# The FFN's down projection: three pairs of row tiles by Strassen's seven products

## The chip, the cores and the metric

The kernel runs on one core of a Trainium2 chip. The metric is device time in microseconds (us) from one launch: TensorE (PE) multiplies matrices, VectorE (DVE) and ScalarE (ACT) work on tiles, GpSimd (POOL) adds at the side, and the queues of SyncE (SP) and ScalarE issue DMA transfers. A profiled execution of the same program gives the trace.

## The reference

Two layers of a decoder trunk, in float32, with 512 positions and width 1024. What the change touches is the second half of each layer and its surroundings:

```python
for l in range(DEPTH):                       # 2
    h = rmsnorm(x, norm_mix[l])
    ...                                      # four mixers, output projection, x = x + ...
    h = rmsnorm(x, norm_ffn[l])
    u = causal_dwconv(h @ ffn_up[l], ffn_dw[l], ffn_dw_b[l])     # 1024 -> 2 * 2816, 3 taps
    gate, val = split_cols(u, [2816, 2816])
    x = x + (silu(gate) * val) @ ffn_down[l]                     # 2816 -> 1024
return rmsnorm(x, norm_final)
```

## The kernel before, in words

Everything is kept transposed: a tile has 128 channels on the partitions and the 512 positions as columns. The residual `x` is eight such tiles. Products run in fp16 with a high and a low part of each operand: `mm3` (lines 231 to 236) issues three matmuls for one 128 x 128 weight block, high by high, high by low, low by high, and sums them in PSUM.

A weight piece is at most 128 x 1024 float32. `w_load` loads it from SP's queue into a staging buffer `st`; `_split` then makes its high part on ScalarE (line 211) and its low part on VectorE (line 212), both into `hl`. There are two staging buffers and five `hl` in the small ring; inside the FFN a second ring `fst`/`fhl` in the FFN's own pool adds two and four, and the third field of an item says which ring it takes. `weights` lists all pieces in order of use, `next_w` keeps `depth` of them split ahead of the one in use (2 in FFN up, 4 at the changes of stage), and splits are traced with high priority. All instructions are put in order per engine when the program is built, by a planner that goes through a simulated timeline with priorities; each engine then takes its own in that order.

FFN up (`ffn_up`): 22 pairs of row tiles, a gate tile and a value tile, each 8 blocks x 3 matmuls of 512 columns into one PSUM bank `g` (two of them). Lines 1103 to 1105 evacuate a bank with the three taps; lines 1109 to 1111 make silu(gate) * value; lines 1113 and 1114 split it into the high and low part of one `act` chunk of 128 x 512. The first four tiles come from `gemm_head`, which runs them in column halves behind the norm.

FFN down (`project`): for each of eight row tiles, 22 chunks x 3 matmuls into one bank; line 1028 (`back`) adds the result to `x`, and `norm_add` squares it for the next norm (ScalarE, then a sum on POOL). The last tile runs in two halves of 256 columns, so that the norm of the first half, or the output of the second layer (`finish`), can start while the second half is multiplied.

Of the kernel before, what the change touches and what calls it, by code (L numbers as in the profile page):

```python
# [40 lines left out]

FST, FHL = 2, 4
# [106 lines left out]
class Builder:  # L149
    def __init__(self, ctx, tc, a):  # L150
# [13 lines left out]
        self.ffn = self.spare = False  # L164
# [25 lines left out]
    def w_load(self, src, cols, ring):  # L190
        nc = self.nc
        if ring:
            st = self.fp.tile([128, 1024], F32, tag="fst", bufs=FST, name=self.n("st"))
        else:
            st = self.wst.tile([128, 1024], F32, tag="st", name=self.n("st"))
        nc.sync.dma_start(st[:, :cols], src)
        return st

# [4 lines left out]
    def _split(self, src, cols, ring=False):  # L203

        nc = self.nc
        st = self.w_load(src, cols, ring)
        if ring:
            hl = self.fp.tile([128, 2, 1024], F16, tag="fhl", bufs=FHL, name=self.n("hl"))
        else:
            hl = self.whl.tile([128, 2, 1024], F16, tag="hl", name=self.n("hl"))  # L210
        act = nc.scalar.activation(hl[:, 0, :cols], st[:, :cols], AF.Copy, scale=SW)  # L211
        dve = nc.vector.scalar_tensor_tensor(hl[:, 1, :cols], st[:, :cols], SW, hl[:, 0, :cols],  # L212
                                             op0=ALU.mult, op1=ALU.subtract)
        for later, earlier in zip((act, dve), self.after):
            self.order(later, earlier)
        return hl
# [14 lines left out]
    def mm3(self, ps, hl, kk, hx, cols, start, stop):  # L231
        nc = self.nc
        w = slice(kk * 128, kk * 128 + 128)
        nc.tensor.matmul(ps, hl[:, 0, w], hx[:, 0, cols], start=start, stop=False)  # L234
        nc.tensor.matmul(ps, hl[:, 0, w], hx[:, 1, cols], start=False, stop=False)  # L235
        nc.tensor.matmul(ps, hl[:, 1, w], hx[:, 0, cols], start=False, stop=stop)  # L236

    def gemm(self, hx):
        if self.stash:
            if self.ffn and len(self.ready) <= self.depth:  # L240
                self.prefetch()
            self.spare = self.ffn
            return self.stash.pop(0)
        hl = self.next_w()

        ps = self.rbank() if self.spare else self.gbank()
        self.spare = False
# [817 lines left out]
    def project(self, rhs, order, tail, scale, norm_eng):  # L1065
        nc = self.nc
        nk = len(order)

        def tile_(ps, hls, cols):
            for i, k in enumerate(order):  # L1070
                self.mm3(ps, hls[k // 8], k % 8, rhs[k], cols, i == 0, i == nk - 1)

        nw = (nk + 7) // 8
        full = slice(0, 512)
        for m in range(NK - tail):
            hls = [self.next_w() for _ in range(nw)]
            ps = self.gbank()
            tile_(ps, hls, full)
            self.back(m, ps, full, scale)
            self.norm_add(m, full, norm_eng)  # L1080
        self.depth = HEAD
        hls = [[self.next_w() for _ in range(nw)] for _ in range(tail)]
        for cols in self.HALVES:
            for i in range(tail):
                m = NK - tail + i
                ps = self.gbank()[:, 0:256]
                tile_(ps, hls[i], cols)
                self.back(m, ps, cols, scale)
                self.norm_add(m, cols, nc.vector if m < NK - 1 else None)
            yield cols  # L1090

    def ffn_up(self, fp, hx):
# [3 lines left out]
        acts = []  # L1096
        for i in range(NF):
            us = []
            for half in range(2):
                ch = i + NF * half  # L1100
                ps = self.gemm(hx)
                u = fp.tile([128, 512], F32, tag="u", bufs=4, name=self.n("u"))
# [5 lines left out]
            th = fp.tile([128, 512], F32, tag="fth", bufs=2, name=self.n("fth"))  # L1108
            nc.scalar.activation(th, us[0], AF.Tanh, scale=0.5)
            stt(us[0], th, 1.0, us[0], op0=ALU.add, op1=ALU.mult)  # L1110
            nc.vector.tensor_tensor(us[0], us[0], us[1], op=ALU.mult)  # L1111
            a = fp.tile([128, 2, 512], F16, tag="act", bufs=NF, name=self.n("act"))
            nc.scalar.copy(a[:, 0], us[0])  # L1113
            nc.vector.tensor_tensor(a[:, 1], us[0], a[:, 0], op=ALU.subtract)
            acts.append(a)
        return acts

    def weights(self):
        a = self.a
        items = []  # L1120
        for l in range(L):
# [13 lines left out]
            for m in range(2 * NF):  # L1135
                items.append((a["up"][l, m], 1024, m < HEAD or m % 2 == 1))
            for m in range(NK):
                for g in range(3):
                    k1 = min(8, NF - 8 * g) * 128
                    items.append((a["dn"][l, m, :, 1024 * g:1024 * g + k1], k1, m == NK - 1 or (3 * m + g) % 2 == 1))  # L1140
# [53 lines left out]
    def run(self):  # L1194
# [24 lines left out]
        for l in range(L):  # L1219
            with pool(f"vp{l}") as self.vp, pool(f"rp{l}") as self.rp:  # L1220
                self.mixers(hx, l, src)
            with pool(f"fp{l}") as fp:
                self.fp, self.ffn, self.depth = fp, True, HEAD
                self.norm_begin(fp)
                hf = self.new_hx(fp, "hf")
                for cols in self.out_second(OTAIL):
                    self.norm_apply(self.d["gf"], hf, cols)
                self.gemm_head(hf, HEAD)
                self.depth = 2
                acts = self.ffn_up(fp, hf)  # L1230
# [95 lines left out]
```

## Time and profile before

| | |
|---|---|
| time, median of 3 runs | 1348.35 us (1348.11 to 1351.59) |
| the profiled execution: its own time, its span | 1351.01 us, 1349.2 us |
| TensorE, VectorE, ScalarE, POOL busy | 1301.4, 903.1, 609.9, 117.7 us |
| mean granted clock of TensorE | 0.989 of full speed |
| loaded from HBM | 114.30 MB, 88 GB/s over the span |
| FFN down, first layer: first matmul, first matmul of the last tile's halves | 560.84 us, 660.56 us |

The busy time of an engine is a share of the whole span; what a change in one stage is worth is read in that stage. A matmul is listed with its full duration, although the next one starts before it ends: the distance from one start to the next is what counts.

### The profile page before, as it was taken

The page shows a single profiled execution, that of the slowest core. Times are in us where ns is not written, and L with a number is a line of the kernel's source. Part 1 is how long each engine was busy: PE and PEld are TensorE (multiplying, and loading weights), DVE is VectorE, ACT ScalarE, POOL GpSimd, SP SyncE. Part 2 cuts the span into 40 slices and gives each one's busy share as a digit, 9 for nine tenths or more (in the row PEclk, how much of TensorE's full clock was granted, in tenths as well). Part 3 has the DMA queues.
Part 4 walks back from the last instruction along what each step waited for, and adds up shares of the span by engine and source line. Part 5 has one row for each costly group of instructions (what it writes and reads, how often), then busy time and mean ns, then how long its engine had stood idle before and what let it go on. Part 6 is the DMA issues. An engine that isn't in the chain of part 4 may idle for free.

```text
span 1349.2 us, 22863 instructions
## 1 busy us (share of the span) xinstructions
PE 1301.4 (96%) x9198; PEld 738.1 (55%) x9198; DVE 903.1 (67%) x1770; ACT 609.9 (45%) x1115; POOL 117.7 (9%) x180
## 2 busy tenths in 40 slices
PE   5999999999999999999999998999999999999996
PEld 4545567657644444444674455775584444444445
DVE  6779985677876767732276899757768666666313
ACT  4544557654544444532154345766345444444210
POOL 2000022223000000001000001223020000000110
PEclk9999999999999999999998999998999999999998
DMA  6421310023223233453133223001213333336201
GB/s 221 157 85 60 118 33 10 1 71 110 78 94 110 94 109 95 141 167 121 52 101 107 80 78 103 10 3 32 94 51 109 107 96 108 96 103 188 70 28 63
DMA packets 41864, 119.96 MB, mean 89 GB/s; under 512 B 4896, under 2 KB 11680, under 8 KB 41760
## 3 DMA queue, kind: packets, MB, share of 16 engines
q1 hardware_dynamic: 35136, 110.50, 25.9%
q10 hardware_dynamic: 6624, 8.01, 1.8%
q8 instruction: 72, 1.18, 0.4%
q14 instruction: 32, 0.26, 0.1%
HBM read 114.30 MB, written 4.19 MB: 88 GB/s over the span
## 4 chain that ended last, share of the span: by engine, by line
PE 81%; DVE 12%; ACT 2%; DMA 2%; issue 2%; SPq 0%; DVEq 0%; ACTq 0%
PE g L234 21%; PE g L235 21%; PE g L236 21%; DVE cacc L755 4%; PE v L922 3%; PE t L911 2%; DVE hl L212 2%; PE s L891 2%; PE r L578 1%; PE r L234 1%; PE r L235 1%; PE r L236 1%; DVE e L894 1%; DMA st<-in_wi_dram 1%; ACT e L898 1%
## 5 line engine op out<-in xcount | busy, mean ns | idle before, releaser
L236 PE MATMUL g<-hx,hl 128*128 128x512 f16 (+1 forms) x1008 | 368.6, 367 | 0.0
L234 PE MATMUL g<-hx,hl 128*128 128x512 f16 (+1 forms) x1008 | 367.8, 367 | 0.8 <-DVE q L787 0.8
L235 PE MATMUL g<-hx,hl 128*128 128x512 f16 (+1 forms) x1008 | 368.2, 367 | 0.3 <-DVE hx L423 0.3
L212 DVE SCALAR_TENSOR_TENSOR hl<-st,hl 128x1024 f16<-128x1024 f32 (+2 forms) x200 | 238.6, 1195 | 115.8 <-ACT hl L211 114.2
L211 ACT ACTIVATE hl<-st 128x1024 f16<-128x1024 f32 (+2 forms) x200 | 204.4, 1026 | 213.4 <-PE g L236 149.3
L234 PEld LDWEIGHTS <-hl 128*128 128x128 f16 x1724 | 170.1, 99 | 159.5 <-issue 5.2
L236 PEld LDWEIGHTS <-hl 128*128 128x128 f16 x1724 | 169.3, 98 | 157.0 <-issue 2.2
L235 PEld LDWEIGHTS <-hl 128*128 128x128 f16 x1724 | 169.6, 98 | 154.2 <-issue 2.5
L235 PE MATMUL g<-act,hl 128*128 128x512 f16 (+1 forms) x396 | 140.7, 355 | 0.0
L236 PE MATMUL g<-act,hl 128*128 128x512 f16 (+1 forms) x396 | 140.7, 355 | 0.0
L234 PE MATMUL g<-act,hl 128*128 128x512 f16 (+1 forms) x396 | 140.7, 355 | 0.0
L1104 DVE SCALAR_TENSOR_TENSOR u<-g,d_fdw,u 128x511 f32<-128x511 f32 x82 | 61.5, 750 | 95.7 <-ACT u L1103 95.7
L1103 ACT ACTIVATE u<-g,par,d_fdw 128x512 f32<-128x512 f32 x82 | 63.7, 777 | 101.6 <-PE g L236 101.4
L755 DVE SCALAR_TENSOR_TENSOR cacc<-gl,d_cdw,cacc 128x511 f32<-128x511 f32 (+14 forms) x120 | 90.0, 750 | 1.3
L1028 DVE SCALAR_TENSOR_TENSOR x<-g,x 128x512 f32<-128x512 f32 (+1 forms) x62 | 34.9, 568 | 83.3 <-PE g L236 83.1
L909 POOL TENSOR_SCALAR e<-e,den 128x512 f32<-128x512 f32 (+3 forms) x96 | 55.9, 595 | 316.4 <-DVE den L901 207.4
L390 POOL TENSOR_TENSOR acc<-acc,sq 128x256 f32<-128x256 f32 (+1 forms) x38 | 41.7, 1098 | 462.4 <-ACT sq L383 405.5
L894 DVE CUSTOM_DVE_ANT_0 e<-s,con 128x512 f32<-128x512 f32 (+3 forms) x96 | 46.8, 488 | 34.2 <-PE s L891 24.4
L1113 ACT CAST act<-u 128x512 f16<-128x512 f32 x44 | 27.1, 617 | 93.2 <-DVE u L1111 93.2
L1105 DVE SCALAR_TENSOR_TENSOR u<-g,d_fdw,u 128x510 f32<-128x510 f32 x82 | 61.4, 748 | 2.8
L898 ACT ACTIVATE e<-e,mx 128x512 f32<-128x512 f32 (+3 forms) x96 | 53.1, 556 | 17.0 <-DVE mx L896 16.9
L383 ACT ACTIVATE sq<-x 128x256 f32<-128x256 f32 (+1 forms) x54 | 24.5, 467 | 74.9 <-DVE x L1028 71.1
(265 smaller groups left out, 1665.0 us busy)
## 6 DMA issues: line engine op xcount, KB each, us to landing
st<-in_up_dram SPq DMA_DIRECT2D x88, 512.0 KB, 3.5
st<-in_wi_dram SPq DMA_DIRECT2D x40, 512.0 KB, 3.4
st<-in_dn_dram SPq DMA_DIRECT2D x32, 512.0 KB, 3.7
st<-in_wo_dram SPq DMA_DIRECT2D x16, 512.0 KB, 3.5
st<-in_dn_dram SPq DMA_DIRECT2D x16, 384.0 KB, 3.2
w<-in_cw_dram ACTq DMA_DIRECT2D x16, 256.0 KB, 4.4
st<-in_wv_dram SPq DMA_DIRECT2D x8, 396.0 KB, 3.2
x<-in_x_dram SPq DMA_DIRECT2D x16, 128.0 KB, 3.4
```

The source lines that it names most:

```text
L211: act = nc.scalar.activation(hl[:, 0, :cols], st[:, :cols], AF.Copy, scale=SW)
L212: dve = nc.vector.scalar_tensor_tensor(hl[:, 1, :cols], st[:, :cols], SW, hl[:, 0, :cols], op0=ALU.mult, op1=ALU.subtract)
L234: nc.tensor.matmul(ps, hl[:, 0, w], hx[:, 0, cols], start=start, stop=False)
L235: nc.tensor.matmul(ps, hl[:, 0, w], hx[:, 1, cols], start=False, stop=False)
L236: nc.tensor.matmul(ps, hl[:, 1, w], hx[:, 0, cols], start=False, stop=stop)
L755: nc.vector.scalar_tensor_tensor(acc[:, s:512], gl[:, 0:512 - s], wj, acc[:, s:512], op0=ALU.mult, op1=ALU.add)
L894: nc.vector.tensor_tensor_reduce(es[i], ps[:, o:o + w], mask[:, 384 - 128 * t:512], op0=ALU.add, op1=ALU.max, scale=1.0, scalar=-3e38, acc ...
L898: nc.scalar.activation(es[i], es[i], AF.Exp, scale=SC, bias=mx[:, i:i + 1], accum_out=den[:, i:i + 1])
L909: nc.gpsimd.tensor_scalar(es[i], es[i], den[:, i:i + 1], 1.0, op0=ALU.mult, op1=ALU.mult)
L1103: act = nc.scalar.activation(u, ps, AF.Identity, scale=w[:, 88 + ch:89 + ch], bias=self.p("fb", ch))
L1104: stt(u[:, 1:512], ps[:, 0:511], w[:, 44 + ch:45 + ch], u[:, 1:512], op0=ALU.mult, op1=ALU.add)
L1105: dve = stt(u[:, 2:512], ps[:, 0:510], w[:, ch:ch + 1], u[:, 2:512], op0=ALU.mult, op1=ALU.add)
```

## The change

Rows and inner dimension of the down product are cut in two: a pair of row tiles (m, m+1) and the even and odd chunks of the 2816 inner channels. With the columns in two halves of 256, a pair is a 2 x 2 product of blocks, and Winograd's form of Strassen's scheme computes it in seven products of 11 chunks, where the plain form has eight. The operands are sums:

- of weights: `make_sums` loads all four quarters A11, A12, A21, A22 of a piece again, and makes S1 to S4 from them with four `tensor_tensor`. For the first two parts of the first pair the loads go by SP's queue into the idle `hx` buffers and the sums run on POOL, inside `ffn_up`; for the rest the loads go by ScalarE's queue into ten `dw` buffers and the sums run on VectorE.
- of activations: `act_pair` holds the two products of chunks 2i and 2i+1 in `q`, as four quarters of 256 columns, makes T1 to T4 on VectorE, and splits quarters and T's into high and low parts (1024 columns each time).

The results need no sums of their own: the seven products are added up inside PSUM, and `back` adds the state of a bank to a quarter of `x` after each product. The pieces of the first pair are 4, 4 and 3 chunks long, those of the others 6 and 5. Three pairs go this way. The last two row tiles stay plain, as one full tile and one in halves, with an order set between their matmuls; half of their `hl` take `dw` buffers. The second ring is gone: the FFN's first four up weights are loaded through the small ring's staging and are split into `act` buffers. `hf`, `u`, `fth`, `q` move to a pool that ends with FFN up, and the output tiles take `dw` buffers. The host reorders `ffn_down` by quarters.

```diff
-    def w_load(self, src, cols, ring):
...
+    def w_pair(self, home):
+        if home == "act":
+            return self.fp.tile([128, 2, 1024], F16, tag="act", bufs=NF // 2, name=self.n("hl"))
+        if home == "dw":
+            return self.dp.tile([128, 2, 768], F16, tag="dw", bufs=DW, name=self.n("hl"))
+        return self.whl.tile([128, 2, 1024], F16, tag="hl", name=self.n("hl"))
...
+    def act_pair(self, fp, q):
+        nc = self.nc
+        a = fp.tile([128, 2, 8 * 256], F16, tag="act", bufs=NF // 2, name=self.n("act"))
+        src = q.rearrange("p a b -> p (a b)")
+        def split(cols):
+            nc.scalar.copy(a[:, 0, cols], src)
+            nc.vector.tensor_tensor(a[:, 1, cols], src, a[:, 0, cols], op=ALU.subtract)
+        def sub(o, i, j):
+            nc.vector.tensor_tensor(q[:, o % 4], q[:, i % 4], q[:, j % 4], op=ALU.subtract)
+        split(slice(0, 1024))
+        sub(self.T1, self.Q12, self.Q11)
+        sub(self.T3, self.Q22, self.Q12)
+        sub(self.T2, self.Q22, self.T1)
+        sub(self.T4, self.Q21, self.T2)
+        split(slice(1024, 2048))
+        return a
+    FAST = {"P1": ("A11", Q11), "P2": ("A12", Q21), "P3": ("S4", Q22), "P4": ("A22", T4), "P5": ("S1", T1),
+            "P6": ("S2", T2), "P7": ("S3", T3)}
+    PARTS = (((0, 4), (4, 8), (8, 11)),) + (((0, 6), (6, 11)),) * 3
+    def fast_order(self, mp):
+        n = range(len(self.PARTS[mp]))
+        if mp:
+            return [(p, h) for p in ("P1", "P5", "P6", "P3", "P7", "P2", "P4") for h in n]
+        raw = ("P1", "P2", "P4")
+        return ([(p, h) for p in raw for h in n[:-1]] + [(p, n[-1]) for p in raw] +
+                [(p, h) for p in ("P5", "P6", "P3", "P7") for h in n])
...
+    def make_sums(self, l, mp, h):
+        nc = self.nc
+        b = {}
+        for name in ("A22", "A11", "A21", "A12"):
+            src, n = self.quarter(l, mp, name, h)
+            if mp == 0 and h < 2:
+                t = self.hxp.tile([128, 512], F32, tag="hx", bufs=NK, name=self.n("dq"))
+            else:
+                t = self.dp.tile([128, 768], F32, tag="dw", bufs=DW, name=self.n("dw"))
+            b[name] = t[:, :n]
+            (nc.scalar if mp or h == 2 else nc.sync).dma_start(b[name], src)
+        tt = (nc.gpsimd if mp == 0 and h < 2 else nc.vector).tensor_tensor
+        tt(b["A22"], b["A21"], b["A22"], op=ALU.add)
+        tt(b["A21"], b["A11"], b["A21"], op=ALU.subtract)
+        tt(b["A11"], b["A22"], b["A11"], op=ALU.subtract)
+        tt(b["A12"], b["A12"], b["A11"], op=ALU.subtract)
+        self.sums[mp, h] = {"S1": b["A22"], "S2": b["A11"], "S3": b["A21"], "S4": b["A12"]}
+    def project_fast(self, l, acts, scale, norm_eng):
+        c1, c2 = self.HALVES[1], self.HALVES[0]
+        with self.tc.high_priority():
+            self.make_sums(l, 0, 2)
+        ahead = {0: {9: 0, 15: 1}, 1: {5: 0, 9: 1}, 2: {}}
+        for mp in range(NK // 2 - 1):
+            m = 2 * mp
+            parts, order = self.PARTS[mp], self.fast_order(mp)
+            x = {"11": (m, c1), "12": (m, c2), "21": (m + 1, c1), "22": (m + 1, c2)}
+            A, B, C = self.gbank()[:, 0:256], self.rbank()[:, 0:256], self.rbank()[:, 0:256]
+            reg = {"P1": A, "P2": B, "P3": C, "P4": A if mp else self.rbank()[:, 0:256], "P5": C, "P6": A, "P7": A}
+            adds = {"P1": ("11",), "P2": ("11",), "P5": ("22",), "P6": ("12",), "P3": ("12",),
+                    "P7": ("22",) if mp else ("22", "21"), "P4": ("21",)}
+            seen = set()
+            for step, (p, h) in enumerate(order):
+                if step in ahead[mp]:
+                    self.make_sums(l, mp + 1, ahead[mp][step])
+                r = reg[p]
+                q = 256 * self.FAST[p][1]
+                k0, k1 = parts[h]
+                hl = self.next_w()
+                for k in range(k0, k1):
+                    self.mm3(r, hl, k - k0, acts[k], slice(q, q + 256), k == k0 and id(r) not in seen,
+                             k == k1 - 1, True)
+                seen.add(id(r))
+                if h < len(parts) - 1:
+                    continue
+                for o in adds[p]:
+                    self.back(x[o][0], r, x[o][1], scale)
...
 in ffn_up:
+            if i in (NF - 8, NF - 5):
+                self.make_sums(l, 0, int(i == NF - 5))
+            if i == NF - 2:
+                self.depth = 4
...
+            if i % 2 == 0:
+                q = up.tile([128, 4, 256], F32, tag="q", bufs=1, name=self.n("q"))
+            nc.vector.tensor_tensor(q[:, 2 * (i % 2):2 * (i % 2) + 2].rearrange("p a b -> p (a b)"), us[0], us[1],
+                                    op=ALU.mult)
+            if i % 2:
+                acts.append(self.act_pair(fp, q))
```

## Rows read from the trace of the kernel before

**Rows 1.** The page's first part: busy us (share of the span), instructions.

```profile
PE 1301.4 (96%) x9198; PEld 738.1 (55%) x9198; DVE 903.1 (67%) x1770; ACT 609.9 (45%) x1115; POOL 117.7 (9%) x180
```

**Rows 2.** The page's chain that ended last: shares of the span by engine.

```profile
PE 81%; DVE 12%; ACT 2%; DMA 2%; issue 2%; SPq 0%; DVEq 0%; ACTq 0%
```

**Rows 3.** TensorE's waits, 300 to 680 us: total, times, longest.

```profile
PE s L403 <- ACT sq L383: 0.4, 1, 0.4
PE g L234 <- DVE x L1028: 0.2, 1, 0.2
```

**Rows 4.** Stretches: length, busy us (instructions) by engine; TensorE's clock, DMA share, GB/s.

```profile
400.00:500.00 100.00, 100.00 (x465) 45.36 (x464) 68.65 (x87) 45.70 (x60) 0.00 (x0) 1.00 0.33 105
560.80:586.00 25.20, 25.20 (x118) 11.45 (x117) 15.36 (x16) 12.43 (x15) 1.12 (x1) 1.00 0.73 236
```

**Rows 5.** TensorE's timeline, first layer's FFN down: start, us, instruction.

```profile
560.84 0.38 PE L234 MATMUL g<-act,hl 128*128 128x512 f16 x1
...
660.56 0.27 PE L234 MATMUL g<-act,hl 128*128 128x256 f16 x1
...
667.76 0.50 PE L403 MATMUL s<-ones,acc 128*128 128x1 f32 x4
```

**Rows 6.** Groups by line and shape, VectorE, then ScalarE: busy us, mean ns, idle.

```profile
L212 DVE SCALAR_TENSOR_TENSOR hl<-st,hl 128x1024 f16<-128x1024 f32 x176 | 215.8, 1227 | 88.9 <-ACT hl L211 87.3 <-PE g L236 1.2
...
L1111 DVE TENSOR_TENSOR u<-u,u 128x512 f32<-128x512 f32 x44 | 30.2, 687 | 0.0
...
L423 DVE TENSOR_TENSOR hx<-nt,hx 128x256 f16<-128x256 f32 x64 | 26.1, 426 | 0.5
...
L1028 DVE SCALAR_TENSOR_TENSOR x<-g,x 128x256 f32<-128x256 f32 x28 | 11.6, 420 | 26.8 <-PE g L236 26.6
...
L211 ACT ACTIVATE hl<-st 128x1024 f16<-128x1024 f32 x176 | 184.5, 1050 | 155.9 <-PE g L236 98.8 <-DMA st<-in_wi_dram 19.9 <-DMA st<-in_dn_dram 14.6
```

**Rows 7.** VectorE's timeline at the end of FFN up: start, us, instruction.

```profile
521.87 1.22 DVE L212 SCALAR_TENSOR_TENSOR hl<-st,hl 128x1024 f16<-128x1024 f32 x1
523.00 0.69 DVE L1111 TENSOR_TENSOR u<-u,u 128x512 f32<-128x512 f32 x1
...
561.85 0.75 DVE L1104 SCALAR_TENSOR_TENSOR u<-g,d_fdw,u 128x511 f32<-128x511 f32 x1 [1.91 <-ACT u L1103]
...
563.30 0.95 DVE L212 SCALAR_TENSOR_TENSOR hl<-st,hl 128x768 f16<-128x768 f32 x1
564.17 0.78 DVE L1111 TENSOR_TENSOR u<-u,u 128x512 f32<-128x512 f32 x1
```

**Rows 8.** ScalarE's timeline, an evacuation, and later a DMA issue (ACTq).

```profile
561.04 0.78 ACT L1103 ACTIVATE u<-g,par,d_fdw 128x512 f32<-128x512 f32 x1 [2.11 <-PE g L236]
...
604.51 0.33 ACTq L1242 DMA_DIRECT2D xs<-x  x1
```

**Rows 9.** DMA issues by line, 340 to 550, then 560 to 590: landing us.

```profile
st<-in_up_dram SPq DMA_DIRECT2D x36, 512.0 KB, 3.5
...
st<-in_dn_dram SPq DMA_DIRECT2D x1, 384.0 KB, 3.0
...
st<-in_dn_dram SPq DMA_DIRECT2D x3, 384.0 KB, 4.3
```

**Rows 10.** A stretch of the convolution stage, columns as in rows 4.

```profile
100.00:120.00 20.00, 19.93 (x125) 10.86 (x124) 19.51 (x35) 8.27 (x18) 0.00 (x0) 1.00 0.25 74
```

**Rows 11.** VectorE's waits, 560 to 590 us.

```profile
DVE hl L212 <- ACT hl L211: 8.1, 6, 4.2
...
DVE hl L212 <- PE g L236: 1.2, 1, 1.2
```

**Rows 12.** Timelines of VectorE and POOL at 318 us; POOL's group of one shape.

```profile
318.79 1.68 DVE L212 SCALAR_TENSOR_TENSOR hl<-st,hl 128x1024 f16<-128x1024 f32 x1
...
318.65 2.40 POOL L390 TENSOR_TENSOR acc<-acc,sq 128x256 f32<-128x256 f32 x2 [0.38 <-ACT sq L383]
...
L1005 POOL TENSOR_TENSOR sq<-sq,sq 128x512 f32<-128x512 f32 x4 | 5.1, 1272 | 26.5 <-ACT sq L1004 26.5
```

More of the change, by code (lines that the diff above doesn't have):

```diff
@@ L201, in w_split, with _split @@
             return self._split(*item)
-    def _split(self, src, cols, ring=False):
+    def _split(self, src, cols, home=None):
         nc = self.nc
[L206 to L214, printed above, removed]
+        st = src() if callable(src) else self.w_load(src, cols)
+        hl = self.w_pair(home)
+        hi = nc.scalar.activation(hl[:, 0, :cols], st[:, :cols], AF.Copy, scale=SW)
+        lo = nc.vector.scalar_tensor_tensor(hl[:, 1, :cols], st[:, :cols], SW, hl[:, 0, :cols],
+                                            op0=ALU.mult, op1=ALU.subtract)
+        for later, earlier in zip((hi, lo), self.after):
             self.order(later, earlier)
@@ L1063, in out_second @@
             yield cols
-    def project(self, rhs, order, tail, scale, norm_eng):
+    Q12, Q11, Q22, Q21, T3, T1, T2, T4 = range(8)
+    def act_pair(self, fp, q):
         nc = self.nc
-        nk = len(order)
-        def tile_(ps, hls, cols):
[L1070 to L1080, printed above, removed]
+        a = fp.tile([128, 2, 8 * 256], F16, tag="act", bufs=NF // 2, name=self.n("act"))
[12 more added lines that the diff above has]
+        return a
@@ new lines, in quarter, with down_items @@
+    def quarter(self, l, mp, name, h):
+        k0, k1 = self.PARTS[mp][h]
+        i, j = self.RAW[name]
+        return self.a["dn"][l, 2 * mp + i, j, :, 128 * k0:128 * k1], 128 * (k1 - k0)
+    def down_items(self, l):
+        items = []
+        for mp in range(NK // 2 - 1):
+            for p, h in self.fast_order(mp):
+                w = self.FAST[p][0]
+                src, n = self.quarter(l, mp, w if w in self.RAW else "A11", h)
+                if w not in self.RAW:
+                    src = lambda w=w, key=(mp, h): self.sums[key][w]
+                items.append((src, n))
+        for w in ("A11", "A12", "A21", "A22"):
+            for h in range(2):
+                items.append(self.quarter(l, NK // 2 - 1, w, h) + (("dw",) if w[1] == "2" else ()))
+        return items
@@ L1081, in project @@
         self.depth = HEAD
-        hls = [[self.next_w() for _ in range(nw)] for _ in range(tail)]
+        m += 1
+        hls = [self.next_w() for _ in range(4)]
         for cols in self.HALVES:
[L1084 to L1089, printed above, removed]
+            ps = self.gbank()[:, 0:256]
+            first, end = tile_(ps, hls, cols)
+            self.order(first, done)
+            done = end
+            self.back(m, ps, cols, scale)
+            self.norm_add(m, cols)
@@ L1135, in weights @@
             for m in range(2 * NF):
[L1136 to L1140, printed above, removed]
+                items.append((a["up"][l, m], 1024, "act" if m < HEAD else None))
+            items += self.down_items(l)
         return items
@@ L1236, in run @@
                 self.norm_begin(fp)
[L1237 to L1243 removed]
+                with pool(f"dp{l}") as self.dp:
+                    for cols in self.project_fast(l, acts, 1.0 / (SW * SA), nc.gpsimd):
+                        if last:
+                            self.finish(self.dp, cols)
+                        else:
+                            for k in range(NK):
+                                nc.scalar.dma_start(src[:, k, cols], self.x[k][:, cols])
+                            self.norm_apply(self.d["gm"], hx, cols)
     def finish(self, pool, cols):
```

96 lines of the change are left out of this document (55 added, 41 removed).

## The prediction

> **What bounds the kernel now.** The first part of the page comes first: TensorE is busy 1301.4 of 1349.2 us, 96% [rows 1]. The chain of waits then says whether that busy time is the path: 81% of it is PE, almost all of it the three matmul lines of `mm3`, 12% VectorE [rows 2]. Third, TensorE's own waits: from 300 to 680 us, which holds the whole FFN of the first layer, it waited 0.6 us [rows 3]. So in both FFNs an us of matmul time taken away is an us of span, until something else becomes late. What could is read from the busy time by stage [rows 4]: in the middle of FFN up VectorE is busy 68.65 of 100 us and DMA moves 105 GB/s; in the first 25 us of FFN down VectorE 15.36 us and DMA 236 GB/s, because there the deep ring fills. TensorE runs at the full granted clock in both.
>
> **Matmuls.** A layer's down product is now 7 row tiles of 66 matmuls over 512 columns, from 560.84 to 660.56 us: 99.72 us for 462, 0.2158 each [rows 5]. The eighth tile runs in column halves, 66 matmuls of 256 columns from 660.56 to 667.76: 0.1091 each, so a half-width matmul costs just half, its weight load beside it. The change leaves that tile and one full tile (66 x 0.2158 = 14.25 us), and makes six tiles into three pairs of 7 products x 11 chunks x 3 = 231 matmuls of 256 columns (25.2 us a pair, 3.60 a product): 693 x 0.1091 = 75.6. Saved: 99.72 - 14.25 - 75.6 = 9.87 us a layer, 19.7 in two.
>
> **VectorE in FFN up.** Per two chunks (20.7 us) come four differences of 256 columns (0.43 each, as the nearest row L423 [rows 6]) and 1024 columns more to subtract for the low parts: two splits of 1024 (start to start 1.13 [rows 7]) for two of 512 (0.69). That is 1.7 + 0.9 = 2.6 us, 13 points: 69% becomes 82%. A result bank is free 0.3 + 0.78 + 1.5 us after its last matmul (evacuation by L1103 to L1105 [rows 7, 8]) and is wanted after 24 x 0.2158 = 5.18, so VectorE may be 2.6 us late for nothing. I cost it 0; without that cover, each us beyond is a us. ScalarE gets 0.9 us per two chunks (two casts of 1.05 for two of 0.62), POOL eight sums.
>
> **The small rings.** Staging drops from four buffers to two and split weights from nine to five. In FFN up a weight tile lasts 5.18 us; its staging buffer is taken for a load (3.5 us), a ScalarE cast (1.05) and a VectorE split (1.23), 5.8 us [rows 6, 9], two at a time: one per 2.9 us. Hidden twice over. The first four up weights have their split space apart and 9 us until the first matmul that needs them: 0, at worst one load of 3.5.
>
> **VectorE at the start of FFN down** is where the sum is made. A 768-column split is 0.87 start to start [rows 7], so 1.02 ns a column: 0.74, 0.61 and 0.48 for 640, 512 and 384. Count from the first down matmul to the second pair's fourth product (25.2 + 3 x 3.60 = 36.0 us):
> last chunks' evacuation, product, four differences, two splits: 1.5 + 0.69 + 1.7 + 2.3 = 6.2;
> splits of the first pair that aren't ready yet, 10 of 512 and 7 of 384: 9.5, and of four products of the second pair, 4 x 1.61 = 6.4;
> sums for the third part (4 x 0.55, by the tensor_tensor L1111, 0.69 at 512 [rows 6]) and for the second pair (4 x (0.95 + 0.82)): 9.2;
> 11 additions to x of 256 columns at 0.42: 4.6.
> In all 35.9 of 36.0 us, where the first 25 us now hold 15.36. So VectorE is full there, then has air: the second and third pair together need 11.3 us of splits and 2.9 of additions each and 7.1 of sums once. A full VectorE need not stop TensorE: in the convolution stage it is busy 19.51 of 20 us while TensorE is busy 19.93 [rows 10]. But there is no such row with splits that feed the very next matmuls. Bounds: nothing, and from the stretch 560 to 590 us, where VectorE stood 9.3 of 30 us behind ScalarE's cast or a buffer [rows 11]; that share of 36 us is 11 us a layer. I am nearer the convolution row: 2.5% of 36 us (0.9), 1.2 us in which the last evacuation hasn't reached VectorE (ScalarE's starts at 561.04, VectorE's at 561.85 [rows 7, 8], after matmuls that end around 560.84), and 1 us for weights. These: the first pair uses nine plain weight pieces in a row, 1.31 us each, then 0.98. Five split buffers keep four ahead. Piece 8 takes piece 6's staging buffer, and piece 6 is split when piece 1 has left its split buffer (2.6 us) and 1.1 us of cast and split are over, 3.7; with a load of 3.0 to 4.3 us (quiet, and in the busy stretch [rows 9]) and 1.1 for cast and split it is there at 7.8 to 9.1, wanted at 9.8. That stands only while nothing is queued ahead of it on VectorE; hence the 1 us. Together 3.1 us a layer, 6.2 in two.
>
> **ScalarE's queue.** It gets 20 loads a layer at 0.33 us of issue [rows 8], 6.6 us, while it works some 10.5 of each 25.2 us: room. A load that waits for a buffer holds every cast behind it, and VectorE and TensorE behind those; by the rotation of ten, the buffers wanted at each of the four later places belong to sums whose splits are issued before, so I take 0; one missed would cost a load, 3 to 4 us. A pair moves 7 quarters of 0.72 MB in 25.2 us, 200 GB/s, where 236 GB/s was moved at 0.73 of the DMA engines [rows 4]. The fixed order of the last two tiles is the one TensorE has now: 0. The output's new buffers are free in time: 0.
>
> **Sum.** -19.7 + 6.2 = -13.5 us. The profiled execution took 1351.01 us (span 1349.2 and 1.8 around it), which gives 1337.5; the median of the three runs is 2.66 lower, so 1334.8.
>
> **A rule weighed.** While POOL adds, VectorE's split at 318.79 took 1.68 us for 1.22 [rows 12], 0.46 more; eight POOL sums would cost VectorE 3.7 us over some 83 us of FFN up, in which it has 15 to spare. The Trainium skill, page "SBUF — State Buffer", section "Who interferes with whom", says that a VectorE instruction with two SBUF inputs and a GpSimd one that reads SBUF exclude each other for the whole instruction. The row shows part of that; what the full rule makes of the time is rival 4.
>
> **Rivals.**
> 1. No new stall: the gain comes whole, 1348.35 - 19.7 = 1328.6. For it: the waits of FFN now are 0.6 us; against it: the 35.9 of 36.0.
> 2. VectorE bounds the first two pairs: at the rate between my share and the upper end, 7 us a layer, 1348.35 - 19.7 + 14 = 1342.6. For it: the row of 9.3 us in 30; against it: that idle time was there because nothing was urgent.
> 3. Slower: the accumulator in PSUM. Products 1, 6, 7 and 4 share a bank (in the first pair 4 has its own) and 5 and 3 another; each may go on only after VectorE has added the state so far to x. That is 11 places a layer, each with one product (3.60 us) of cover for 0.3 + 0.42. It decides when VectorE's queue is over 2.9 us long, as with a group of four sums (3.8) ahead of the addition. At 4.1 us each place costs 1.2, 13 us a layer: 1355. Break-even is 0.9 us a place. Against it: only some places meet a group.
> 4. POOL and VectorE take turns for whole instructions in FFN up. Four sums of 1.27 us [rows 12] in 10.4 us block VectorE for 5.1, of which 1.9 is spare and 2.6 is the bank's cover: 0.6, four times, 1337.2. The Trainium skill's page is the one named above.
> 5. The change doesn't pay as counted: where weights change every 0.109 us for 75 us on end, half-width matmuls come at 0.123, which eats all: 1348. Against it: rows 5 show 66 in a row.
>
> **Chances.** Forecast (1.5 to 5 us of stall a layer, 1331.6 to 1338.7) 0.50, rival 1 0.20, rival 2 0.14, rival 3 0.08, rival 4 0.05, rival 5 0.03. What can be told from no change is about 0.3%, 4 us. Faster than 1344.3: 0.50 + 0.20 + 0.05 + 0.11 of rival 2, 0.86; within: the rest of rival 2 and most of 5, 0.05; slower 0.09. The range goes from a little below rival 1 to past rival 2, 1327 to 1345, and leaves rivals 3 and 5 and the tails out, some 15%.
>
> **What would show it.** Right: 1386 matmuls of 256 columns more or less 0.109 apart in both down stages, PE waits of about 3 us a layer there, in the first two pairs, on VectorE's hl or ScalarE's cast; VectorE 95% busy in the first 36 us and 80 to 85% in FFN up with no PE wait. Rival 3 would show as waits of `mm3` for L1028's x, rival 4 as waits for u in FFN up, a late load as ScalarE's wait for st. Wrong is the forecast if the waits in down pass 5 us a layer or are absent, or if other stages move by more than 3 us.

## The result: 1.1% slower

The changed kernel took 1362.76 us in the median of four runs (1361.22 to 1365.43), the kernel before 1349.25 beside it: a ratio of 1.011, 95% interval 1.0093 to 1.0127. I had forecast 1334.8. The profiled run took 1361.43 us with a span of 1359.6, 10.4 more than before.

The first part of the page after and its chain, which answer to [rows 1] and [rows 2]:

```profile
PE 1290.3 (95%) x9792; PEld 797.1 (59%) x9792; DVE 1034.9 (76%) x1996; ACT 657.9 (48%) x1181; POOL 137.0 (10%) x196
...
PE 70%; DVE 16%; DMA 6%; ACT 3%; issue 2%; POOL 2%; SPq 0%; ACTq 0%; DVEq 0%; POOLq 0%
```

TensorE has less to do and is the path for 70% of the span instead of 81%: something else became late. Its waits from 300 to 680 us, where [rows 3] had 0.6 us:

```profile
PE s L410 <- POOL acc L397: 4.8, 2, 4.1
PE r L234 <- ACT hl L210: 3.8, 1, 3.8
PE g L234 <- DVE x L1035: 2.8, 3, 1.8
PE t L414 <- DVE y L294: 1.2, 1, 1.2
PE g L236 <- DVE hl L211: 0.8, 2, 0.6
...
```

Where the time went is read from the starts of four kinds of matmuls in TensorE's timeline (the first of the output projection's halves, the first full-width one of FFN up, the first half-width one of the last tile, the last one of FFN down). Length of each stretch in us, and in brackets the difference to the kernel before; the two columns on the right are experiments told below:

| stretch | before | after | all fixes (e8) | e8 without sums (e11) |
|---|---|---|---|---|
| to the projection's halves, layer 1 | 314.31 | 314.96 (+0.65) | 312.04 (-2.27) | 316.54 (+2.23) |
| norm before FFN up, layer 1 | 39.33 | 42.59 (+3.26) | 40.03 (+0.70) | 40.11 (+0.78) |
| FFN up, pairs, tile 6, layer 1 | 306.92 | 307.94 (+1.02) | 302.73 (-4.19) | 297.95 (-8.97) |
| last tile, layer 1 | 15.02 | 21.06 (+6.04) | 16.53 (+1.51) | 15.84 (+0.82) |
| mixers, layer 2 | 299.67 | 296.78 (-2.89) | 298.06 (-1.61) | 298.29 (-1.38) |
| norm before FFN up, layer 2 | 39.31 | 42.83 (+3.52) | 40.84 (+1.53) | 39.93 (+0.62) |
| FFN up, pairs, tile 6, layer 2 | 306.92 | 305.08 (-1.84) | 301.69 (-5.23) | 297.95 (-8.97) |
| last tile and tail, layer 2 | 27.72 | 28.36 (+0.64) | 28.38 (+0.66) | 28.49 (+0.77) |
| span | 1349.2 | 1359.6 (+10.4) | 1340.3 (-8.9) | 1335.1 (-14.1) |

The third and seventh lines should each have become 9.87 us shorter, so they lost 10.9 and 8.0 us. With 6.8 us in the two norm stages and 6.0 at the last tile that is 31.7 us, more than the 19.7 saved. (The mixers' lines, which the change does not touch, differ by up to 3 us between single profiles.)

**The pairs.** TensorE's, VectorE's and ScalarE's timeline in the first pair (start, us, instruction; in brackets the idle time before it and what ended it):

```profile
578.75 0.27 PE L236 MATMUL r<-act,hl 128*128 128x256 f16 x1
582.82 0.40 PE L234 MATMUL r<-act,hl 128*128 128x256 f16 x1 [3.80 <-ACT hl L210]
...
584.05 0.42 PE L234 MATMUL r<-act,hl 128*128 128x256 f16 x1
...
588.10 0.42 PE L234 MATMUL g<-act,hl 128*128 128x256 f16 x1
...
588.47 0.27 PE L236 MATMUL g<-act,hl 128*128 128x256 f16 x1
...
577.36 1.23 DVE L1085 TENSOR_TENSOR act<-q,act 128x1024 f16<-128x1024 f32 x1 [0.78 <-ACT act L1084]
...
581.59 0.56 DVE L1148 TENSOR_TENSOR dw<-dw,dw 128x384 f32<-128x384 f32 x1 [2.10 <-DMA dw<-in_dn_dram]
...
576.29 1.04 ACT L1084 CAST act<-q 128x1024 f16<-128x1024 f32 x1 [2.13 <-DVE q L1088]
...
576.99 4.87 ACTq L1146 DMA_DIRECT2D dw<-in_dn_dram  x8
```

The last row joins eight loads. Listed from 577.5 on, without the first of them, it begins at:

```profile
578.62 3.23 ACTq L1146 DMA_DIRECT2D dw<-in_dn_dram  x7
```

Read backwards: TensorE waits 3.80 us for the first split of a third-part sum; the sum waits for its quarters. The first of the four loads is asked for only at 576.99, since on ScalarE's queue it stands behind a cast that itself waited 2.13 us for VectorE. The other three come out from 578.62 on, just after VectorE's last reading of q (L1085, 577.36 + 1.23 = 578.59), where their buffers lie. From 582.8 to 588.3 matmuls run at the lower of the clock's two levels, 1.2 GHz: 19 of them from 584.05 to 588.10, 0.213 apart and no longer 0.109. The 27 matmuls from 582.82 to 588.57 took 5.75 us, 2.8 more than at 0.109; some 0.2 of that are two short waits for splits, so the lower clock cost about 2.6 us. The second layer has the same pause, 3.76 us, and by the same count 2.8 us behind it. Stretches, columns as in [rows 4]:

```profile
400.00:500.00 100.00, 100.00 (x466) 45.28 (x464) 81.47 (x109) 49.21 (x58) 0.00 (x0) 1.00 0.34 101
559.60:595.60 36.00, 31.45 (x236) 23.74 (x235) 26.70 (x44) 15.35 (x25) 0.85 (x1) 0.91 0.50 162
```

FFN up is as forecast: VectorE 81.47 of 100 us, TensorE never idle. In the second row the granted clock is 0.91 in the mean. In the 36 us that I had filled with 35.9 us of VectorE's work it is busy 26.70: late, not full.

**The norm stage.** POOL's and VectorE's timeline while FFN up's input is normed:

```profile
339.53 1.33 POOL L1149 TENSOR_TENSOR dq<-dq,dq 128x512 f32<-128x512 f32 x1
340.94 1.40 POOL L1150 TENSOR_TENSOR dq<-dq,dq 128x512 f32<-128x512 f32 x1
342.42 1.28 POOL L1151 TENSOR_TENSOR dq<-dq,dq 128x512 f32<-128x512 f32 x1
...
339.66 1.23 DVE L284 TENSOR_SCALAR ti<-u 128x2 int32<-128x2 int32 x1
...
341.14 1.23 DVE L285 TENSOR_SCALAR y<-ti 128x2 int32<-128x2 int32 x1
342.40 0.16 DVE L288 TENSOR_TENSOR a<-y 128x2 f32<-128x2 f32 x1
342.60 1.11 DVE L289 SCALAR_TENSOR_TENSOR a<-a,u 128x2 f32<-128x2 f32 x1
```

The eight POOL sums are written late in FFN up, but nothing ties them there; the planner put them into the norm stage, 162 and 170 us ahead of where e1 runs them (313.84 and 338.19 against 476.16 and 507.79). There VectorE computes a reciprocal root in operations on two columns. Three of them take 1.1 to 1.2 us, and each ends within 0.04 us of a POOL sum's end (339.53 + 1.33 = 340.86 against 339.66 + 1.23 = 340.89). The one that starts in POOL's gap at 342.40 takes 0.16. Of TensorE's waits listed above, the 1.2 us for y (L294) are this chain; the second layer has 1.4. The first four sums cost something on POOL's own queue too: the norm's additions (L397) start right behind them, and TensorE waits for those:

```profile
320.01 6.27 POOL L397 TENSOR_TENSOR acc<-acc,sq 128x512 f32<-128x512 f32 x6
...
326.34 0.61 PE L410 MATMUL s<-ones,acc 128*128 128x1 f32 x4 [0.72 <-POOL acc L397]
```

**The last tile of the first layer:**

```profile
670.43 1.23 DVE L211 SCALAR_TENSOR_TENSOR hl<-st,hl 128x1024 f16<-128x1024 f32 x1 [3.12 <-ACT hl L210]
672.97 1.23 DVE L211 SCALAR_TENSOR_TENSOR hl<-st,hl 128x1024 f16<-128x1024 f32 x1 [1.31 <-ACT hl L210]
674.11 0.69 DVE L1035 SCALAR_TENSOR_TENSOR x<-g,x 128x512 f32<-128x512 f32 x1
...
675.66 1.26 POOL L397 TENSOR_TENSOR acc<-acc,sq 128x512 f32<-128x512 f32 x1 [17.11 <-ACT sq L390]
...
676.98 0.91 PE L410 MATMUL s<-ones,acc 128*128 128x1 f32 x4 [4.11 <-POOL acc L397]
```

Tile 6 is done at about 665.5. Its addition (L1035) stands in VectorE's order behind two splits of the next layer's weights, which wait for loads, and runs 8.6 us later; the square, POOL's sum and TensorE's norm matmul follow it one by one.

### The profile page after: what moved, and what is told of

The parts are those of the page before. It is cut to its first block, busy times and chain, and to the rows that moved or that the text cites. A ratio compares the mean times of both kernels' runs of the same rounds, so it can differ in the third digit from the quotient of the medians.

```text
span 1359.6 us, 24589 instructions
## 1 busy us (share of the span) xinstructions
PE 1290.3 (95%) x9792; PEld 797.1 (59%) x9792; DVE 1034.9 (76%) x1996; ACT 657.9 (48%) x1181; POOL 137.0 (10%) x196
## 3 DMA queue, kind: packets, MB, share of 16 engines
HBM read 127.28 MB, written 4.19 MB: 97 GB/s over the span
## 4 chain that ended last, share of the span: by engine, by line
PE 70%; DVE 16%; DMA 6%; ACT 3%; issue 2%; POOL 2%; SPq 0%; ACTq 0%; DVEq 0%; POOLq 0%
PE g L234 17%; PE g L236 16%; PE g L235 16%; DVE cacc L762 4%; DVE hl L211 3%; PE v L929 3%; DMA st<-in_dn_dram 2%; PE r L234 2%; PE r L235 2%; PE r L236 2%; PE t L918 2%; PE s L898 2%; PE r L585 1%; DMA st<-in_wi_dram 1%; ACT hl L210 1%
## 5 line engine op out<-in xcount | busy, mean ns | idle before, releaser
L211 DVE SCALAR_TENSOR_TENSOR hl<-st,hl 128x1024 f16<-128x1024 f32 (+5 forms) x210 | 233.4, 1113 | 85.5 <-ACT hl L210 85.2
L210 ACT ACTIVATE hl<-st 128x1024 f16<-128x1024 f32 (+5 forms) x210 | 199.9, 953 | 174.6 <-PE g L236 61.3
L234 PEld LDWEIGHTS <-hl 128*128 128x128 f16 x1922 | 190.6, 99 | 143.3 <-ACT hl L210 9.1
L236 PEld LDWEIGHTS <-hl 128*128 128x128 f16 x1922 | 189.7, 99 | 136.3 <-issue 3.5
L235 PEld LDWEIGHTS <-hl 128*128 128x128 f16 x1922 | 189.9, 99 | 133.4 <-issue 6.5
L234 PE MATMUL g<-act,hl 128*128 128x256 f16 (+1 forms) x374 | 109.0, 292 | 1.9 <-DVE x L1035 1.8
L236 PE MATMUL g<-act,hl 128*128 128x256 f16 (+1 forms) x374 | 109.0, 291 | 0.8 <-DVE hl L211 0.8
L235 PE MATMUL g<-act,hl 128*128 128x256 f16 (+1 forms) x374 | 108.9, 291 | 0.0
L397 POOL TENSOR_TENSOR acc<-acc,sq 128x256 f32<-128x256 f32 (+1 forms) x38 | 39.0, 1026 | 431.1 <-ACT sq L390 430.3
L1085 DVE TENSOR_TENSOR act<-q,act 128x1024 f16<-128x1024 f32 x44 | 53.8, 1223 | 20.2 <-ACT act L1084 20.2
L1084 ACT CAST act<-q 128x1024 f16<-128x1024 f32 x44 | 45.7, 1038 | 46.2 <-DVE q L1242 42.0
L234 PE MATMUL r<-act,hl 128*128 128x256 f16 x220 | 60.8, 277 | 7.6 <-ACT hl L210 7.6
L1035 DVE SCALAR_TENSOR_TENSOR x<-g,x 128x256 f32<-128x256 f32 (+1 forms) x74 | 36.4, 499 | 37.8 <-PE g L236 37.6
```

Of the source, the lines that this page charges most:

```text
L210: hi = nc.scalar.activation(hl[:, 0, :cols], st[:, :cols], AF.Copy, scale=SW)
L211: lo = nc.vector.scalar_tensor_tensor(hl[:, 1, :cols], st[:, :cols], SW, hl[:, 0, :cols], op0=ALU.mult, op1=ALU.subtract)
L234: first = nc.tensor.matmul(ps, hl[:, 0, w], hx[:, 0, cols], start=start, stop=False, **kw)
L236: return first, nc.tensor.matmul(ps, hl[:, 1, w], hx[:, 0, cols], start=False, stop=stop, **kw)
L1085: nc.vector.tensor_tensor(a[:, 1, cols], src, a[:, 0, cols], op=ALU.subtract)
```

## The experiments

Ratios are to the kernel before, run beside them on the same chip, with 95% intervals; the changed kernel's is 1.011. The edits are shown shortened.

**e1: the POOL sums tied to FFN up.**

```
+ self.gate = nc.gpsimd.tensor_scalar(g, th[:, 0:8], 1.0, None, op0=ALU.mult)   # at i = NF-8, NF-5
- tt(b["A22"], b["A21"], b["A22"], op=ALU.add)
+ s1 = tt(b["A22"], b["A21"], b["A22"], op=ALU.add); self.order(s1, self.gate)
```

> The eight GpSimd sums of the first two parts are tied behind a small GpSimd operation that reads a chunk late in FFN up, so that they run there and no longer in the norm stage ahead of FFN up. Theory (three separate losses: sums in the norm stage 7.5 us, third part's late sums 8 to 12 us, last tile 5.9 us): the half-square markers of the norm stage come back to the pace of the kernel before, in both layers, and the time falls by 7.5 us from 1362.8, to about 1355. VectorE's tiny operations of the norm fall from 1.1 to 1.2 us back to 0.16 us. Rival (VectorE is simply full, and the losses are spread by its load): the sums only move the loss, FFN up or the first pair loses what the norm stage gains, and the time stays within 2 us of 1362.8.

1.0071 (1.0045 to 1.0096): 5.3 us less, of 7.5 expected. The two norm stretches are 0.79 and 1.77 us over the kernel before, where they were 3.26 and 3.52. VectorE's timeline at the same place, then in FFN up beside POOL's sums (507.79 to 513.7):

```profile
336.09 0.16 DVE L284 TENSOR_SCALAR ti<-u 128x2 int32<-128x2 int32 x1
...
507.97 1.76 DVE L1243 SCALAR_TENSOR_TENSOR u<-fth,u 128x512 f32<-128x512 f32 x1
509.65 2.89 DVE L1088 TENSOR_TENSOR q<-q 128x256 f32<-128x256 f32 x2
```

The sums hold VectorE there as well (0.68 and 0.75 us without them), 3.2 us for this group and 1.4 for the one before it, but the slack takes it: TensorE does not wait. The rival falls. What is left in the norm stretches is a wait for an addition to x, 0.9 us in the first layer and 1.9 in the second, where the kernel before has 0.2 in each. In the second layer the addition stands on VectorE behind the split of one of FFN up's first weights, which came late:

```profile
983.51 1.06 ACT L210 ACTIVATE hl<-st 128x1024 f16<-128x1024 f32 x1 [1.78 <-DMA st<-in_up_dram]
...
984.60 1.23 DVE L211 SCALAR_TENSOR_TENSOR hl<-st,hl 128x1024 f16<-128x1024 f32 x1 [1.80 <-ACT hl L210]
985.75 0.75 DVE L1035 SCALAR_TENSOR_TENSOR x<-g,x 128x256 f32<-128x256 f32 x2
...
986.22 0.27 PE L234 MATMUL g<-y,hl 128*128 128x256 f16 x1 [1.89 <-DVE x L1035]
```

**e2, e5, e6: the third part's loads.** e2 changes their queue, e5 the place of their buffers, e6 both.

```
e2 - (nc.scalar if mp or h == 2 else nc.sync).dma_start(b[name], src)
   + (nc.scalar if mp else nc.sync).dma_start(b[name], src)
e5 + for tag, shape, bufs in (("fth", [128, 512], 2), ("u", [128, 512], 4), ("q", [128, 4, 256], 1)):
   +     up.tile(shape, F32, tag=tag, bufs=bufs, name=self.n(tag))    # ahead of hf: q no longer lies under these dw
   + names[-1:] + names[:-1] if mp == 0 and h == 2 else names         # A12 first
```

> The four loads of the third part's weight sums are issued from SyncE's queue instead of ScalarE's, nothing else changes. Theory: they are issued some us earlier, no longer behind a cast that waits for VectorE and a store that waits for a tile's finish; the pause of 3.8 us in TensorE ahead of the fifth product goes, and the half clock of 2.3 us behind it: 6 us for each layer, the time falls by 8 to 12 us, to about 1352. Rival (VectorE full): the sums come earlier, but VectorE's splits are then later, the pause turns up at another product, and the time falls by less than 2 us. Rival (the buffers come free late, whichever queue asks): the loads land no earlier and nothing changes.

> The third part's four quarters are placed where FFN up's input lay, whose last reader is a matmul at about 565, and no longer where the activation pairs' f32 tile q lies, whose last reader is VectorE at 575.2; their loads stay on ScalarE's queue. Theory of the third part now (two conditions in a row: the place is free only after the last split of the activations, and ScalarE's in-order queue gives the loads out only behind the cast at 576.3): place alone does nothing, since the queue still holds them until 576.6, 0.4 us earlier than in the changed kernel; time within 2 us of 1362.8. Rival (the place alone is the cause): the loads land before 578 and the pause of 3.8 us and the half clock behind it go, 8 to 12 us in two layers.

> The place of e5 and SyncE's queue of e2 together, nothing else. Theory: the loads are issued at about 571 without a wait and land by 575, so that the sums stand before TensorE needs the third piece of the fifth product at 578.75; the pause (3.8 us) and the half clock behind it (2.3 us) go in both layers: 10 to 12 us, about 1351 to 1353. Rival (VectorE is full there, 0 idle between 565 and 600): the sums are ready earlier but the activations' last splits are later by as much, and less than 4 us are won.

e2: 1.014 (1.012 to 1.0159), slower still, and its last rival is why. SyncE's and TensorE's waits in e2's first pairs, then TensorE's in e5 and in e6:

```profile
SPq L1146 <- DVE act L1085: 4.1, 1, 4.1
...
PE r L234 <- ACT hl L210: 8.2, 1, 8.2
```

```profile
PE r L234 <- ACT hl L210: 4.9, 1, 4.9
```

```profile
PE r L234 <- ACT hl L210: 2.6, 1, 2.6
```

The place is free only when VectorE has read q for the last time (L1085), and the pause doubles: the second pair's loads, no longer behind those of the third part on ScalarE's queue, are given out in front of three of them, and theirs take up to 6.9 us to land. e5, the place: the pauses stay (4.9 and 3.8 us), 1.0084 (1.0063 to 1.0105), an interval that overlaps the changed kernel's. Its loads are given out from 574.08 on, no longer held by L1085, which ends at 575.68; but e5 also loads A12 first, so that the sum waits for the fourth load, which took 4.2 us to land, and no longer for the third, which took 2.5 in the changed kernel. The place with the old order of loads was not run. e6, both: pauses of 2.6 and 2.2 us, 1.0061 (1.004 to 1.0082), 6.6 us less; I had expected 10 to 12. What is left is still a late load. SyncE's and VectorE's timeline in e6:

```profile
572.69 1.85 SPq L1147 DMA_DIRECT2D dw<-in_dn_dram  x4
...
578.55 0.56 DVE L1149 TENSOR_TENSOR dw<-dw,dw 128x384 f32<-128x384 f32 x1 [0.49 <-DMA dw<-in_dn_dram]
```

I had expected the four loads at 571 and landed by 575. They stand on SyncE's queue behind two loads of plain weights, come out from 572.69 on and take 4.0 us in the median. So neither queue nor place alone gained anything that these runs can tell, and together they remove a third of the pause or a little more, not all of it.

**e3: tile 6's addition ahead of the next layer's splits.**

```
+ dve = self.back(m, ps, full, scale)           # and self.sq = the square of norm_add
+ self.depth = 0                                # while the last tile's weights are taken
+ self.after = self.sq, dve
+ self.depth = HEAD; prefetch up to HEAD
```

> The first splits of the next layer's input weights are ordered behind the finish and the square of the last but one tile, so that this finish no longer stands on VectorE behind splits that wait for a load. Theory: in the first layer the last tile's 4.1 us wait for the sum of squares goes, with the half clock of 1.3 us behind it; the time falls by 5 to 6 us, to about 1357. Rival (the loads of the next layer's weights are late and TensorE waits for them instead): the 4 to 6 us turn up at the next layer's first matmuls, and the time stays within 2 us of 1362.8.

1.0065 (1.0043 to 1.0086): 6.1 us less. VectorE's and POOL's timeline: the addition follows at once, POOL is done long before the norm matmul, and the weights come no later.

```profile
662.20 0.68 DVE L1036 SCALAR_TENSOR_TENSOR x<-g,x 128x512 f32<-128x512 f32 x1
665.60 1.23 DVE L211 SCALAR_TENSOR_TENSOR hl<-st,hl 128x1024 f16<-128x1024 f32 x1 [2.71 <-ACT hl L210]
...
663.75 1.27 POOL L398 TENSOR_TENSOR acc<-acc,sq 128x512 f32<-128x512 f32 x1 [10.12 <-ACT sq L390]
```

**e4 (e1 + e2 + e3) and e7 (e1 + e3 + e6).**

> All three edits together. Theory (three separate losses): they add up, 7.5 + 8 to 12 + 5.9, and the time is 1337 to 1342, faster than the kernel before by 0.5 to 0.9%, with what is left of the forecast gain of 19.7 us eaten by small stalls in the pairs. Rival (VectorE full, one cause): removing places of loss makes others, and the time stays above 1350.

> Place and queue of e6, with the ties of e1 and e3. Theory (separate losses that add): 10 to 12 us below the kernel with all three edits but the old place had those gains without its longer pause: 1347.4 x 1.011 = 1362.2 for the changed kernel on this chip, less 5.3 (e1), 6.1 (e3) and 10 to 12, so 1339 to 1341, a ratio of 0.994 to 0.995 to the kernel before. Rival (the pauses come back elsewhere): above 1347, not faster.

e4: 1.0076 (1.0047 to 1.0104), 1356.31 us: the rival's number, but not for its reason, since e2's part is itself a loss; the single differences add to 1.011 - 0.0039 - 0.0045 + 0.003 = 1.0056, inside the interval. e7: 0.999 (0.9973 to 1.0008), 1347.33 us, not told from no change; the sum with e6's part, -0.0049, is 0.9977. Within the intervals the losses are separate and add; the expected 0.994 fails with e6's shortfall.

**e8: e7, with the sixth product's first pieces ahead of the fifth's third.**

```
- [(p, h) for p in ("P5", "P6", "P3", "P7") for h in n]
+ [(p, h) for g in (n[:-1], n[-1:]) for p in ("P5", "P6") for h in g] + [(p, h) for p in ("P3", "P7") for h in n]
```

> As e7, and the sixth product's first two pieces run ahead of the fifth's third piece in the first pair, which needs the late third sums 2.6 us later. Theory: if e7 still shows a pause ahead of the fifth's third piece, this takes up to 2.6 us of it for each layer; if e7 shows none, no change against e7 (within 1 us). Rival (VectorE's order is what counts: the split of the sixth product's pieces then stands ahead of the late sums): slower than e7 by 1 to 3 us.

0.9962 (0.9946 to 0.9977), 1342.97 us: 0.28% below e7, and faster than both kernels, than the one before by 0.4%. TensorE's waits from 550 to 655 us, then the stretch with the largest of them and the one like it in the second layer:

```profile
PE r L234 <- ACT hl L210: 1.3, 1, 1.3
PE r L236 <- DVE hl L211: 0.6, 1, 0.6
...
```

```profile
575.00:600.00 25.00, 22.62 (x190) 18.91 (x189) 22.95 (x38) 12.32 (x19) 1.74 (x1) 0.93 0.72 239
...
1225.00:1260.00 35.00, 31.19 (x283) 27.29 (x282) 32.55 (x54) 17.51 (x27) 2.73 (x1) 1.00 0.73 231
```

**e9 and e12: two more orders on VectorE.** e9 puts the fourth product's addition behind the third sums; e12 also puts the second pair's sums behind the fifth product's addition.

```
e9  + if mp == 0 and p == "P4": self.order(add, self.third)
e12 + if mp == 0 and p == "P5": self.add_up(1, 0, self.quarters, add)
```

> As e8, with one order more: the addition of the fourth product into x stands behind the third part's sums on VectorE, and no longer ahead of them. In e8 VectorE waits 1.87 us with that addition (from 573.6 to 575.5, until the fourth product is done) while the landed quarters lie behind it, and TensorE then waits 1.27 and 0.65 us for their splits. Theory (what is left in the first pair is order in VectorE's queue, not VectorE's time): these waits go, 1.5 to 2 us for each layer, 3 to 4 us below e8: about 1339. Rival (VectorE is full): the addition now comes 2 us later and the next products wait for its bank instead; within 1 us of e8.

> As e9, and the first sum of the second pair, which waits 0.5 us for its load on VectorE ahead of the fifth product's addition, stands behind that addition. In e9 TensorE waits 2.1 and 1.9 us for this addition, which frees the bank of the third product. Theory (order in VectorE's queue): this wait falls to 0.5 us or less, 3 us below e9 in two layers, about 1339. Rival (VectorE full): the second pair's products wait for their sums by as much, within 1 us of e9.

0.9954 (0.9938 to 0.997) and 0.9965 (0.9951 to 0.9978): neither is told from e8, and my theory of the order falls here. TensorE's waits in the first layer's pairs, e9 and then e12:

```profile
PE r L234 <- DVE x L1036: 2.1, 1, 2.1
...
```

```profile
PE r L236 <- DVE hl L211: 1.2, 2, 1.0
PE g L236 <- DVE hl L211: 0.9, 2, 0.6
...
```

The wait that each removes comes back at the next consumer: first the bank, then the splits.

**e10 and e11: the price of the sums.** e10 takes raw quarters through the plain ring and drops the sums' loads (with e3 and e8's order); e11 is e8 with loads, places and splits as they are, and only the additions gone.

> The weight sums S1 to S4 are left out: each product with a sum takes the raw quarter A11 in its place, loaded on SyncE's ring as the other raw quarters are; the number of loads, splits and matmuls stays, the 16 sums on VectorE a pair and ScalarE's loads go (with the order of e3 and e8). It measures what the three pairs cost if sums were free. Theory (the losses left after e8, 5.7 and 4.6 us in the two layers' pairs, come from the sums' place in VectorE's and the queues' order): the pairs come down to 1 us of their matmul time and the time is 8 to 10 us below e8, about 1333. Rival (the additions from PSUM banks or the raw loads hold the pairs): 3 us or less below e8.

> As e8, but the additions that make S1 to S4 are left out, on VectorE and on GpSimd; their quarters are still loaded by the same queues into the same places and split as they come, so the products with a sum run on raw quarters. Loads, splits and matmuls stay. It measures what the sums' own engine time costs (80 VectorE operations of 0.55 to 0.96 us for each layer, counted in the rows as 20 each of four lines, less the GpSimd ones), which e10 did not, since its loads all went through one ring of few places. Theory (in e8 the pairs' remaining loss of 5.7 and 4.6 us comes from VectorE's time and order): the pairs come to within 2 us of their matmul time in each layer, and the time is 6 to 9 us below e8's 1343, about 1335. Rival (loads, banks and activations hold the pairs in any case): less than 3 us below e8.

e10: 1.0396 (1.0375 to 1.0417), the contrary of both expectations, and no measure of the sums. ScalarE's waits from 560 to 690 us:

```profile
ACT hl L210 <- DMA st<-in_dn_dram: 80.4, 45, 3.7
```

All weights of the pairs then come through a ring of two staging buffers, one load after the other; with half-width matmuls that is too slow: FFN up, pairs and tile 6 of the first layer take 26.3 us more than before (352.42 to 685.66 us). It shows what the ten places of the sums' own ring carry. e11: 0.9911 (0.9897 to 0.9924), 0.51% or 6.9 us below e8, as the theory had it. TensorE's waits in the first layer's pairs, and e8's stretch:

```profile
PE r L234 <- DVE x L1036: 0.3, 1, 0.3
...
```

```profile
575.00:600.00 25.00, 24.48 (x224) 21.57 (x222) 18.43 (x30) 14.16 (x21) 1.27 (x1) 1.00 0.94 318
```

DMA moves 318 GB/s there and hinders nothing, and 224 matmuls in 24.48 us are 0.109 each. In both layers the stretch with the pairs comes within 0.9 us of the full saving of 9.87. With the additions their operands' waits go too, so e11 prices both together.

## Why the prediction was wrong

The profiled time is 23.9 us above the 1337.5 that the sum gave for it. Three things that the sum held at 0 make that up: the late load and the clock behind it (6.4 and 6.6 us in the two layers), the POOL sums' place (6.8 in the norm stages, which hold some late up weights too) and the last tile's order (6.0); the other stages took off 1.6, and the rest of FFN up and the pairs came to 5.9 where 6.2 stood.

**Matmuls, -9.87 a layer: right.** Half the columns cost half the time for as long as their operands are there (e11), which settles rival 5.

**FFN up, the small rings: right but for the first weights.** No wait from 350 to 560 us, VectorE at 81% for the forecast 82. The first up weights, put at 0 or at worst one load, were not quite free: with the POOL sums gone (e1, e8, e11) each norm stage is still 0.6 to 1.8 us longer than before, and TensorE's only waits there are for additions to x; in e1's second layer the one of 1.9 us stands behind a late split of an up weight.

**ScalarE's queue, "so I take 0; one missed would cost a load, 3 to 4 us": the step that failed first.** One was missed in each layer, and the price was right: 3.80 and 3.76 us. I followed the rotation of the ten buffers only at the four later places. At the first place the buffers lie where FFN up's tiles were, under the tile that VectorE reads last, and the queue is that of an engine whose cast waits for the same VectorE. I also left out what follows a pause: the lower granted clock, 2.6 and 2.8 us.

**VectorE at the start of FFN down, +3.1 a layer: near in sum, partly by luck.** In the changed kernel the pause and the clock leave 4.5 and 1.4 us of the two layers' losses. What the sums' additions cost in the pairs once the order is mended, their time and the waits for them together, is the difference of e8 and e11: 4.8 and 3.7 us, more than 3.1. The stall I took for late raw weights did not come; no long wait of TensorE in the pairs traces to st. Where "full" was right is narrower than my 36 us: in e8's 575 to 600, right after the sums' late start, VectorE is busy 22.95 of 25 us, and e9 and e12 could only choose who waits. The convolution row [rows 10], to which I leaned, has nothing that feeds the very next matmul; splits do.

**POOL's sums: priced at the wrong place.** I let them run where the program writes them, with 15 us of VectorE's slack beside them. e1 shows that price to be fair (4.6 us of VectorE for the forecast 3.7, none of TensorE). But a planner sets their place. In the norm stage the path runs through VectorE's smallest operations (waits of 1.2 and 1.4 us) and through POOL's own additions (0.7 in each layer). The two stages lost 6.8 us; e1 took 4.2 off them, and 5.3 off the time. This is rival 4's mechanism where I had not looked for it. The rule of the Trainium skill, page "SBUF — State Buffer", section "Who interferes with whom", that an instruction with two SBUF inputs and a GpSimd one that reads SBUF exclude each other fits L289 (1.11 us beside POOL) and L288 (0.16 in its gap). The same section exempts instructions with one SBUF input outside the two-port modes, which it says `tensor_scalar` can enter; L284 and L285 are such and took 1.23 us, and no run here tells in which mode they were.

**"The fixed order of the last two tiles is the one TensorE has now: 0": failed, +6.0 in the first layer.** TensorE's order is indeed the same. What stands before tile 6's addition on VectorE is not, and e3 removes the loss by that order alone. I checked the moved work on one engine's queue and not on the others.

**Rivals.** Rival 3's mechanism shows once in the first layer's pairs, with 1.8 us (the longest wait for L1035), not 13. Rival 2 was nearest for the pairs, yet its 7 us a layer were two things: some 4 for the sums (e8 against e11), and a late load that queue, place and order cure in part. The forecast's own signs of failure came true: other stages moved by over 3 us three times, and the waits in the first layer's FFN down passed 5 us (3.8, 1.8, 0.8 and 0.5).

**What stays open.** No run gives e6's four loads out earlier, ahead of the plain weights on SyncE's queue, or has the first up weights in time for the norm stage, so neither rest is shown to go away. e11 does not part the sums' time on VectorE from the waits for their operands. A faster split, or sums on another engine, were not tried.

## What to carry to other kernels

For work that a change adds, find out who decides its place: a planner may move an untied operation 160 us to where its engine looks idle and where it blocks a chain of tiny operations; tie it to the data of the stage that has the slack. For each new load ask two questions in a row: when does the last reader leave the place where it lands, and which waiting instruction stands in front of it on its queue; curing one alone gained nothing here that could be told. And a cost counted as busy time against a stretch's length says little for work with deadlines: price the operations that stand between data and the next matmul.

## What the runs showed of the hardware

A VectorE operation on two columns went from 0.16 to 1.23 us beside POOL's sums, and ended with them. After a pause of TensorE of 3.80 us matmuls ran at the lower level of the clock, 1.2 GHz, for 5.5 us, which cost about 2.6 us more; after pauses of 2.3 and 2.6 us (e7, granted clock 0.66 and 0.83 in 576 to 586 and 1239 to 1249) it fell as well. In e8's first layer it fell after waits of 1.3 and 0.6 us (0.93 in 575 to 600), while in its second layer waits of 1.3, 0.6 and 1.9 us close together left it at 1.00. The four loads of 192 KB for the third part landed in 2.4 to 3.7 us in the changed kernel's first layer; in e2 three of them, given out behind four of 384 KB, took 6.9.
